# Strassen's seven products for three quarters of the MLP's way down, sums kept in SBUF

## The chip, the cores and the metric

One core of one Trainium2 chip runs the whole program in one launch. The metric is device time in microseconds, the median of three runs. Five engines with queues of their own matter: TensorE (PE; its weight loads are listed as PEld), VectorE (DVE), ScalarE (ACT), GpSimd (POOL, which issues weight loads) and SyncE (SP, which issues the other transfers).

## The reference, cut to what matters

Two layers on 512 tokens of width 1024. Each is a mixer (three attention branches, gates, an output projection) and an MLP with a hidden width of 4096:

```
x = x + mixer(rmsnorm(x, g_mix[l])) 
h = rmsnorm(x, g_mlp[l])
x = x + square(relu(h @ w_up[l])) @ w_down[l]     # 1024 -> 4096 -> 1024
```

After the second layer comes a last RMSNorm. All inputs are float32. The change touches `@ w_down[l]`, what feeds it and what takes its result.

## The kernel before, in words

Activations lie channel-major: a tile has 128 channels on the partitions and the 512 tokens (`S`) along the row. Every float32 product is made of three matmuls in fp32r: each operand is split into a high part (a ScalarE copy with rounding) and a low part (a VectorE subtraction), and `mm3` adds high*high, high*low and low*high in PSUM. `wblock` loads a block of weights of 128 x 1024 words through POOL's queue into a `raw` tile and splits it into a pair of `w` tiles.

The program isn't issued in the order in which it is written. `Plan` records every operation, and `Plan.schedule` (line 306) then places them by a list schedule with costs of its own: on each engine the ready operation that was written earliest goes first, if its tiles fit. SBUF has 42 slots of 1024 words and 12 of 512 (`n4`, `n2`), PSUM has 8 banks. The limits that matter here: at most 12 `w` tiles and 6 `raw` tiles at once, and a `raw` load at most 350 recorded operations ahead of the first one that isn't placed yet (`limits`, `ahead`). A tile is given a slot only if the operations written before it still find room for theirs (`fits`). Every instruction is emitted from one line, 562, so groups are told apart by tile names.

The MLP (from `mark("mlp")`, line 1546) runs in two halves of the hidden width. In each, 16 chunks of 128 hidden channels are made: 24 matmuls of 512 columns on `h`, a Relu on ScalarE, a product on VectorE that makes the square, and the split into `u` (in slots tagged co, qk, om, v). Then, for each pair of 128-channel output blocks (`mp` 0 to 3), four blocks of `w_down` are loaded and split, two PSUM banks take 48 matmuls of 512 columns each, and VectorE multiplies by the norm's factor `R2` and adds to the residual `xt`, which lies in SBUF from the output projection (`mark("wout")`) on. In the second half of the last layer the last pair is done by halves of 256 tokens, so that the end of the program overlaps with matmuls. The inner loop of the way down reads:

```
for q in range(2):
    for i in range(2):
        wh, wl = wblock(w_down[l], 16 * hf + 8 * q, 8, 256 * mp + 128 * i)
        mm3(pp[i], wh, wl, us[8 * q:8 * q + 8], first=q == 0, last=q == 1)
```

Of the kernel before, what the change touches and what calls it, by code (L numbers as in the profile page):

```python
# [12 lines left out]
F32R = mybir.dt.float32r  # L13
I32 = mybir.dt.int32
AF = mybir.ActivationFunctionType
OP = mybir.AluOpType
# [4 lines left out]
S = 512  # L21
# [7 lines left out]
for _n, _w in ([("dq", 512), ("dk", 512), ("dv", 512)]  # L29
# [13 lines left out]


class View:
# [530 lines left out]
def trunk(ctx, tc, x, w_in, b_gate, g_mix, diff_lambda, g_diff, g_cq, g_ckv, w_uq, w_ukv,  # L576
# [9 lines left out]
    ten, act, dve = plan.tensor, plan.scalar, plan.vector  # L586

    def mark(label):
        plan.label = label
        plan.boost = opts["boost"] if label == "A" else 0  # L590
    plan.boost = 0

    def T(tag, shape=None, dt=F32):
        if shape is None:
            shape = dict(t=[128, S], th=[128, S], o=[128, S], p=[128, S], pd=[128, 1024], raw=[128, 1024]).get(tag, [128, 2, S])
        return plan.tile(shape, dt, tag)

    def H(tag):
        return T(tag, [128, 2, S], F32R)
# [4 lines left out]
    def P(tag, shape=(128, S)):  # L604
        return plan.bank(shape, tag)

    def dma(dst, src):
        return plan.sync.dma_start(dst, src)

    def copy(dst, src, scale=1.0):  # L610
        return act.activation(dst, src, AF.Copy, scale=scale)
# [17 lines left out]
    p = P("mm")  # L629
# [5 lines left out]
    def load(src, kc, n):  # L635

        v = T("raw")[:, :kc * n].rearrange("p (k n) -> p k n", n=n)
        plan.gpsimd.dma_start(v, src)
        return v

    def wview(w, k0, kc, c0, n):
        return w[k0 * 128:(k0 + kc) * 128, c0:c0 + n].rearrange("(k p) n -> p k n", p=128)

    def pair():

        wh = T("w", [128, 1024], F32R)
        wl = T("w", [128, 1024], F32R)
        plan.together(wh, wl)
        return wh, wl
# [24 lines left out]

    def hilo(dst, src):
        copy(dst[:, 0], src)
        dve.tensor_sub(dst[:, 1], src, dst[:, 0])
# [60 lines left out]
    xs = [plan.dram(dr.tile([128, 2, S], F32, name=f"xs{k}")) for k in range(4)]  # L738
    h = [None] * KD
# [45 lines left out]
    for k in range(KD):  # L785
        p = P("x0")
# [39 lines left out]
    def layer(l, norm):  # L826
# [59 lines left out]
        k0 = 0  # L886
        for kc in (3, 3, 2):
            wh, wl = wblock(W, k0, kc, LAY["ckv"], 288)
            for k in range(kc):
                for b in range(4):  # L890
                    a0, a1 = (h[k0 + k][:, u, 128 * b:128 * b + 128] for u in range(2))
                    o = p4[b][:, :288]
# [9 lines left out]
        s4 = small(4)  # L902
# [8 lines left out]
        r2, v, f = small(4), small(4), small(4)  # L911
# [10 lines left out]
        for k in range(2):  # L922
            p = P("tp")
            for b in range(4):
                ten.transpose(p[:, 128 * b:128 * b + 128], u4[:, b, 128 * k:128 * k + 128], ident)
            c = H("co")
            g = gckv[:, k:k + 1]
# [5 lines left out]
        for a, op in ((0, dve.tensor_sub), (1, dve.tensor_add)):  # L933
            o = kro[:, :, 16 * a:16 * a + 16]
# [3 lines left out]
        p = P("tp")  # L938
# [30 lines left out]
        for pr in range(4):  # L969
            p = P("mm")  # L970
            mm3(p, khw, klw, ckv, c0=128 * pr)
            t = H("rx")
# [25 lines left out]
        for b in range(4):  # L998
            p = P("mm")
            vproj(p, vhw, vlw, ckv, b, 512)  # L1000
            src = p.rearrange("p (r h d) -> p r h d", h=2, d=64)
# [481 lines left out]
        g = {br: [(f"g{br}{m}", 1.0, bind(gate, br, m)) for m in range(8)] for br in range(3)}  # L1483
# [45 lines left out]
        merged = [merged[m] for m in range(KD)]  # L1529

        mark("wout")
        xt = []
        for i in range(4):
            t = T("xt", [128, 2, S])
            dma(t, xs[i])
            xt += [t[:, 0], t[:, 1]]
        n2 = Norm(gmlp)
        for mp in range(4):
            for i in range(2):
                m = 2 * mp + i  # L1540
                wh, wl = wblock(w_out[l], 0, 8, 128 * m)
                p = P("mm")
                mm3(p, wh, wl, merged)
                dve.tensor_add(xt[m], xt[m], p)
                n2.chunk(m, xt[m])
        mark("mlp")
        last = l == NL - 1
        nn = Norm(vec(g_final if last else g_mix[l + 1], KD))
        R2 = None
        for hf in range(2):  # L1550
            us = []
            for jp in range(8):
                for i in range(2):
                    wh, wl = wblock(w_up[l], 0, 8, 2048 * hf + 256 * jp + 128 * i)
                    p = P("mm")
                    mm3(p, wh, wl, h)
                    t = T("t")
                    act.activation(t, p, AF.Relu)
                    dve.scalar_tensor_tensor(t, p, 0.0, t, OP.max, OP.mult)
                    n = len(us)  # L1560
                    u = H("co" if n < 4 else "qk" if n < 10 else "om" if n < 14 else "v")
                    hilo(u, t)
                    us.append(u)
                if hf == 0 and jp == 0:
                    Rt2 = n2.stat(DM)
                    sq = small(4)
                    dve.tensor_mul(sq, Rt2, Rt2)
                    R2 = R
                    copy(R2, spread(sq))
            for mp in range(4):  # L1570
                if last and hf == 1 and mp == 3:
                    break
                pp = [P("mm"), P("mm")]
                for q in range(2):
                    for i in range(2):
                        wh, wl = wblock(w_down[l], 16 * hf + 8 * q, 8, 256 * mp + 128 * i)
                        mm3(pp[i], wh, wl, us[8 * q:8 * q + 8], first=q == 0, last=q == 1)
                for i in range(2):
                    m = 2 * mp + i
                    t = T("t")  # L1580
                    dve.tensor_mul(t, pp[i], R2)
                    dve.tensor_add(xt[m], xt[m], t)
                    if hf == 1:
                        if last:
                            nn.sq(xt[m])
                        else:
                            dma(xs[m // 2][:, m % 2], xt[m])
                            nn.chunk(m, xt[m])
        if not last:
            return nn  # L1590

# [1 line left out]
        for k in range(6):  # L1593
            copy(xt[k], xt[k], scale=nn.g[:, k:k + 1])
        orow = out[0].rearrange("(p r) d -> r p d", r=4)
        ws = [[wblock(w_down[l], 16 + 8 * q, 8, 128 * m) for m in (6, 7)] for q in range(2)]
        for hh in range(2):
            cs = slice(256 * hh, 256 * hh + 256)
            pp = [P("mm")[:, :256], P("mm")[:, :256]]
            for q in range(2):  # L1600
                for i in range(2):
                    mm3(pp[i], *ws[q][i], [u[:, :, cs] for u in us[8 * q:8 * q + 8]], first=q == 0, last=q == 1)
            sums = [nn.acc]
            for i in range(2):
                xm = xt[6 + i][:, cs]
                t = T("t")
                dve.tensor_mul(t[:, cs], pp[i], R2[:, cs])
                dve.tensor_add(xm, xm, t[:, cs])
                sq = T("t")
                act.activation(sq[:, cs], xm, AF.Square)  # L1610
                copy(xm, xm, scale=nn.g[:, 6 + i:7 + i])
                sums.append(sq)
            p = P("tp")
            for n, sq in enumerate(sums):
                for j in range(2):
                    c = 256 * hh + 128 * j
                    ten.matmul(p[:, j:j + 1], sq[:, c:c + 128], ones, start=n == 0 and j == 0, stop=n == 2 and j == 1)
            v = small(2)
            dve.tensor_scalar(v, p[:, 0:2], 1.0 / DM, EPS, op0=OP.mult, op1=OP.add)
            y = rsqrt(v, 2)  # L1620
            for j in range(2):
                r = 2 * hh + j
                ot = T("v", [128, 2, S])
                for q in range(2):
                    p = P("x0")
                    for k in range(4):
                        ten.transpose(p[:, 128 * k:128 * k + 128], xt[4 * q + k][:, 128 * r:128 * r + 128], ident)
                    if q == 0:
                        copy(ot[:, q], p, scale=y[:, j:j + 1])
                    else:  # L1630
                        dve.tensor_scalar(ot[:, q], p, y[:, j:j + 1], None, op0=OP.mult)
                    dma(orow[r][:, S * q:S * q + S], ot[:, q])
# [58 lines left out]
```

## Time and profile before

| what | value |
|---|---|
| runs | 2001.65, 1988.54, 1996.59 us; median 1996.59 |
| the profiled execution | 2001.1 us, span 1999.3 us |
| mean granted TensorE clock | 0.991 |
| instructions | 25782, of them 9652 matmuls |
| busy PE, DVE, ACT, POOL | 1949.1, 1249.1, 836.6, 219.8 us |

In the profile a matmul's recorded end is modelled and matmuls are pipelined, so the pace of a stream is read from start to start in the timeline, not from the mean of one. An engine that is busy all the time shows in a stage's window; an engine's idle time matters only where another one waits for it.

### The profile page before, as it was taken

The page shows a single profiled execution, that of the slowest core. Times are in us where ns is not written, and L with a number is a line of the kernel's source. Part 1 is how long each engine was busy: PE and PEld are TensorE (multiplying, and loading weights), DVE is VectorE, ACT ScalarE, POOL GpSimd, SP SyncE. Part 2 cuts the span into 40 slices and gives each one's busy share as a digit, 9 for nine tenths or more (in the row PEclk, how much of TensorE's full clock was granted, in tenths as well). Part 3 has the DMA queues.
Part 4 walks back from the last instruction along what each step waited for, and adds up shares of the span by engine and source line. Part 5 has one row for each costly group of instructions (what it writes and reads, how often), then busy time and mean ns, then how long its engine had stood idle before and what let it go on. Part 6 is the DMA issues. An engine that isn't in the chain of part 4 may idle for free.

```text
span 1999.3 us, 25782 instructions
## 1 busy us (share of the span) xinstructions
PE 1949.1 (97%) x9652; PEld 1620.4 (81%) x9652; DVE 1249.1 (62%) x2633; ACT 836.6 (42%) x1539; POOL 219.8 (11%) x260
## 2 busy tenths in 40 slices
PE   8899899999999999999999999999999999999998
PEld 7788788887778888888887877888877888888887
DVE  6687867788866533444356977687878754334432
ACT  5465544544434431333243754455434433223321
POOL 1000001000111111211100000001011211111100
PEclk9999999999999999999999999999999999999999
DMA  7944626567653323433257264456667433234211
GB/s 219 200 112 139 188 76 188 166 159 208 171 158 102 97 74 94 117 90 110 79 119 187 72 188 129 127 148 177 167 190 219 130 86 103 74 107 115 83 55 43
DMA packets 191220, 263.17 MB, mean 132 GB/s; under 512 B 97964, under 2 KB 128684, under 8 KB 191096
## 3 DMA queue, kind: packets, MB, share of 16 engines
q1 hardware_dynamic: 154776, 129.14, 24.1%
q0 software_dynamic: 36320, 132.40, 23.4%
q8 instruction: 76, 1.25, 0.3%
q14 instruction: 48, 0.39, 0.1%
HBM read 210.83 MB, written 46.47 MB: 129 GB/s over the span
## 4 chain that ended last, share of the span: by engine, by line
PE 85%; DMA 7%; DVE 5%; ACT 1%; SPq 1%; issue 1%; DVEq 0%; ACTq 0%
PE mm L562 74%; PE s L562 4%; PE tp L562 3%; PE av L562 3%; DMA raw<-in_w_in_dram 2%; DMA raw<-in_w_uq_dram 1%; SPq L562 1%; DVE t L562 1%; DMA sm<-al 1%; DVE w L562 1%; DVE sm L562 1%; DMA al<-sm 1%; DVE oo L562 1%; DVE rx L562 1%; ACT w L562 0%
## 5 line engine op out<-in xcount | busy, mean ns | idle before, releaser
L562 PE MATMUL mm<-h,w 128*128 128x512 f32 x3936 | 970.2, 398 | 0.0
L562 PEld LDWEIGHTS mm<-h,w 128*128 128x128 f32 x3936 | 731.9, 189 | 160.1 <-issue 0.3
L562 DVE TENSOR_TENSOR w<-raw,w 128x1024 fp32r<-128x1024 f32 (+4 forms) x366 | 372.9, 1031 | 120.4 <-ACT w L562 118.2
L562 ACT ACTIVATE w<-raw 128x1024 fp32r<-128x1024 f32 (+4 forms) x366 | 321.9, 901 | 210.0 <-PE mm L562 123.3
L562 PE MATMUL mm<-co,w 128*128 128x512 f32 (+1 forms) x864 | 212.0, 392 | 3.7 <-ACT w L562 3.1
L562 PE MATMUL mm<-qk,w 128*128 128x512 f32 (+1 forms) x900 | 212.0, 385 | 0.0
L562 PE MATMUL mm<-om,w 128*128 128x512 f32 (+1 forms) x792 | 194.9, 388 | 0.0
L562 PEld LDWEIGHTS mm<-qk,w 128*128 128x128 f32 x900 | 164.6, 188 | 36.1
L562 PEld LDWEIGHTS mm<-co,w 128*128 128x128 f32 x864 | 158.5, 189 | 39.5 <-ACT w L562 3.5
L562 DVE TENSOR_TENSOR t<-mm,const 128x512 f32<-128x512 f32 (+1 forms) x114 | 75.3, 677 | 182.3 <-PE mm L562 181.9
L562 PEld LDWEIGHTS mm<-om,w 128*128 128x128 f32 x792 | 144.7, 188 | 32.0 <-issue 0.2
L562 POOL DMA_DIRECT2D raw<-in_w_in_dram x86 | 74.9, 873 | 855.8 <-PE mm L562 313.9
L562 PE MATMUL mm<-w,h 128*128 128x256 f32 (+1 forms) x1152 | 155.8, 287 | 0.0
L562 PEld LDWEIGHTS mm<-w,h 128*128 128x128 f32 x1152 | 149.7, 191 | 3.6 <-DVE w L562 0.4
L562 PE MATMUL s<-qk,qk 96*128 96x512 f32 (+2 forms) x448 | 128.0, 371 | 8.0 <-DVE sm L562 4.2
L562 DVE SCALAR_TENSOR_TENSOR t<-mm,t 128x512 f32<-128x512 f32 x64 | 44.2, 691 | 141.1 <-ACT t L562 141.1
L562 ACT ACTIVATE t<-mm 128x512 f32<-128x512 f32 x74 | 44.2, 597 | 189.8 <-PE mm L562 189.8
L562 ACT ACTIVATE p<-s,sm 128x512 f32<-128x512 f32 x128 | 87.1, 684 | 63.3 <-DVE sm L562 62.9
L562 ACT ACTIVATE pt<-tp 128x512 fp32r<-128x512 f32 x128 | 71.7, 595 | 87.5 <-PE tp L562 85.1
L562 PE MATMUL av<-pt,v 128*128 128x256 f32 x576 | 98.3, 293 | 5.6 <-DVE pt L562 3.4
L562 PEld LDWEIGHTS av<-pt,v 128*128 128x128 f32 x576 | 83.4, 191 | 22.2 <-DVE pt L562 8.0
L562 PEld LDWEIGHTS s<-qk,qk 128*128 128x128 f32 (+1 forms) x448 | 81.3, 192 | 23.5 <-DVE sm L562 5.6
(141 smaller groups left out, 1717.4 us busy)
## 6 DMA issues: line engine op xcount, KB each, us to landing
raw<-in_w_in_dram POOLq DMA_DIRECT2D x80, 512.0 KB, 6.3
raw<-in_w_up_dram POOLq DMA_DIRECT2D x64, 512.0 KB, 4.8
raw<-in_w_down_dram POOLq DMA_DIRECT2D x64, 512.0 KB, 4.8
dk<-rx SPq DMA_DIRECT2D x40, 512.0 KB, 4.9
qk<-dk SPq DMA_DIRECT2D x40, 512.0 KB, 6.5
raw<-in_w_in_dram SPq DMA_DIRECT2D x24, 512.0 KB, 6.8
dq<-rx SPq DMA_DIRECT2D x40, 256.0 KB, 4.5
qk<-dq SPq DMA_DIRECT2D x20, 512.0 KB, 4.4
```

The lines of the kernel that those rows point to most:

```text
L562: getattr(getattr(self.nc, op.eng), op.m)(*args, **kw)
```

## The change

The hidden width of each layer is cut in four quarters. For the first three (`PAIRS = (4, 4, 4)`: three groups of four pairs of hidden chunks) the way down is computed by the Strassen-Winograd scheme. A block problem has two halves of hidden channels (the two chunks of a pair), two halves of output channels (the two blocks of an `mp`) and two halves of tokens. Eight products of 256 columns become seven, made from sums of weight blocks (`ss`) and of activation blocks (`ht`), each of which is split into high and low parts again. The seven products lie in four PSUM banks; after each group they are copied (first group) or added (second and third) into tiles in SBUF (`da`, `db`). `outputs` combines them at the end. The last quarter is done as before, with eight chunks. The residual is written to DRAM in the output projection and read back before the last quarter (`x_back`).

```diff
+PAIRS = (4, 4, 4)
...
+        xm, xt = x_back()
...
+            dma(xs[mp], xm[mp])
...
+        def up_pair(c0):
+            b = T("hb", [128, 2, 2, HB])
+            for i in range(2):
+                wh, wl = wblock(w_up[l], 0, 8, c0 + 128 * i)
+                p = P("mm")
+                mm3(p, wh, wl, h)
+                t = T("t")
+                act.activation(t, p, AF.Relu)
+                act.activation(b[:, i].rearrange("p t n -> p (t n)"), t, AF.Square)
+            t13, t24 = T("ht", [128, 2, HB]), T("ht", [128, 2, HB])
+            dve.tensor_sub(t13[:, 0], b[:, 0, 1], b[:, 0, 0])
+            dve.tensor_sub(t13[:, 1], b[:, 1, 1], b[:, 0, 1])
+            dve.tensor_sub(t24[:, 0], b[:, 1, 1], t13[:, 0])
+            dve.tensor_sub(t24[:, 1], t24[:, 0], b[:, 1, 0])
+            parts = []
+            for src in (b[:, :, 0], t13, t24):
+                u = T("u", [128, 2, 2, HB], F32R)
+                copy(u[:, 0], src)
+                dve.tensor_sub(u[:, 1], src, u[:, 0])
+                parts += [u[:, :, 0], u[:, :, 1]]
...
+            hilo(u, b[:, 1, 1])
+            b11, b21, t1, t3, t2, t4 = parts
+            return [b11, b21, u, t4, t1, t2, t3]
+
+        def down_weights(k0, n, mp):
+            rows = w_down[l][128 * k0:128 * k0 + 256 * n, 256 * mp:256 * mp + 256].rearrange("(j i p) n -> p i j n", i=2, p=128)
+            raw = [load(rows[:, i], n, 256).rearrange("p j (o n) -> p j o n", o=2) for i in range(2)]
...
+            s12, s34 = four(T("ss", [128, 1024])), four(T("ss", [128, 1024]))
+            dve.tensor_add(s12[:, 0], raw[0][:, :, 1], raw[1][:, :, 1])
+            dve.tensor_sub(s12[:, 1], s12[:, 0], raw[0][:, :, 0])
+            dve.tensor_sub(s34[:, 0], raw[0][:, :, 0], raw[0][:, :, 1])
+            dve.tensor_sub(s34[:, 1], raw[1][:, :, 0], s12[:, 1])
+            wh, wl = pair()
+            a1 = [four(w) for w in (wh, wl)]
+            for i in range(2):
+                copy(a1[0][:, i], raw[i][:, :, 0])
+                dve.tensor_sub(a1[1][:, i], raw[i][:, :, 0], a1[0][:, i])
+            a2 = four(T("w", [128, 1024], F32R))
+            copy(a2[:, 0], raw[1][:, :, 1])
+            dve.tensor_sub(a2[:, 1], raw[1][:, :, 1], a2[:, 0])
+            ws = []
+            for s_ in (s12, s34):
+                wh, wl = pair()
+                copy(four(wh), s_)
+                dve.tensor_sub(four(wl), s_, four(wh))
...
+        def product(o, n, ws, us):
+            wh, wl = ws[n]
+            for j, u in enumerate(us):
+                u0, u1 = u[n][:, 0], u[n][:, 1]
+                ten.matmul(o, wh[:, j], u0, start=j == 0, stop=False)
+                ten.matmul(o, wh[:, j], u1, start=False, stop=False)
+                ten.matmul(o, wl[:, j], u0, start=False, stop=j == len(us) - 1)
+
+        BANKS = ((0, 1), (5, 6), (3, 4), (2,))
...
+        def keep(g, mp, pb):
...
+                if g == 0:
+                    copy(d, p)
+                else:
+                    dve.tensor_add(d, d, p)
+
+        def outputs(mp):
+            c = T("hb", [128, 2, 2, HB])
+            p12, p67, p45, p3 = sums[mp]
+            dve.tensor_add(c[:, 0, 0], p12[:, 0], p12[:, 1])
+            dve.tensor_add(p12[:, 0], p12[:, 0], p67[:, 0])
+            dve.tensor_add(p67[:, 0], p12[:, 0], p67[:, 1])
+            dve.tensor_add(p12[:, 0], p12[:, 0], p45[:, 1])
+            dve.tensor_sub(c[:, 1, 0], p67[:, 0], p45[:, 0])
+            dve.tensor_add(c[:, 0, 1], p12[:, 0], p3)
+            dve.tensor_add(c[:, 1, 1], p12[:, 0], p67[:, 1])
...
+        for g, n in enumerate(PAIRS):
+            us = []
+            for j in range(n):
+                us.append(up_pair(256 * (first + j)))
...
+            for mp in range(4):
+                keep(g, mp, down(2 * first, n, mp, us))
+            first += n
+
+        us = [up_chunk(128 * c) for c in range(2 * first, 32)]
+        first *= 2
+        xm, xt = x_back()
+        for mp in range(4):
+            cs = outputs(mp)
+            for i in range(2):
+                m = 2 * mp + i
+                dve.tensor_mul(cs[i], cs[i], R2)
+                dve.tensor_add(xt[m], xt[m], cs[i])
+        for mp in range(4):
+            if last and mp == 3:
+                break
+            pp = [P("mm"), P("mm")]
+            for i in range(2):
+                wh, wl = wblock(w_down[l], first, len(us), 256 * mp + 128 * i)
+                mm3(pp[i], wh, wl, us)
...
-        ws = [[wblock(w_down[l], 16 + 8 * q, 8, 128 * m) for m in (6, 7)] for q in range(2)]
+        ws = [wblock(w_down[l], first, len(us), 128 * m) for m in (6, 7)]
```

## Rows read from the trace of the kernel before

**Rows 1.** Page, span and engines: busy us (share of the span), instructions.
```profile
span 1999.3 us, 25782 instructions
...
PE 1949.1 (97%) x9652; PEld 1620.4 (81%) x9652; DVE 1249.1 (62%) x2633; ACT 836.6 (42%) x1539; POOL 219.8 (11%) x260
```

**Rows 2.** Page, the chain that ended last: shares of the span by engine.
```profile
PE 85%; DMA 7%; DVE 5%; ACT 1%; SPq 1%; issue 1%; DVEq 0%; ACTq 0%
```

**Rows 3.** Windows of layer 0's MLP: stretch, its us, busy us, clock, DMA, GB/s.
```profile
655.00:745.00 90.00, 90.00 (x393) 72.82 (x392) 39.51 (x61) 33.02 (x47) 11.73 (x14) 1.00 0.30 82
...
745.00:835.00 90.00, 90.00 (x390) 72.91 (x389) 33.91 (x37) 20.51 (x21) 16.77 (x19) 1.00 0.40 110
```

**Rows 4.** Timeline of PE, 512-column matmuls on the way down: start us, us, count.
```profile
985.45 2.94 PE L562 MATMUL mm<-qk,w 128*128 128x512 f32 x12
988.23 2.93 PE L562 MATMUL mm<-co,w 128*128 128x512 f32 x12
991.00 4.34 PE L562 MATMUL mm<-qk,w 128*128 128x512 f32 x18
```

**Rows 5.** Timeline of PE, 256-column matmuls on the way down, near the end.
```profile
1978.38 1.58 PE L562 MATMUL mm<-qk,w 128*128 128x256 f32 x12
1979.80 1.58 PE L562 MATMUL mm<-co,w 128*128 128x256 f32 x12
```

**Rows 6.** Groups by form, PE, whole span: busy us, mean ns, idle before.
```profile
L562 PE MATMUL mm<-w,h 128*128 128x256 f32 x960 | 127.9, 283 | 0.0
```

**Rows 7.** Timeline of DVE in the output projection, instructions back to back.
```profile
596.99 0.68 DVE L562 SCALAR_TENSOR_TENSOR th<-th,mm 128x512 f32<-128x512 f32 x1
597.70 0.69 DVE L562 TENSOR_TENSOR co<-co,th 128x512 f32<-128x512 f32 x1
...
598.91 1.22 DVE L562 TENSOR_TENSOR w<-raw,w 128x1024 fp32r<-128x1024 f32 x1
600.04 0.68 DVE L562 SCALAR_TENSOR_TENSOR qk<-co,qk 128x512 fp32r<-128x512 f32 x1
600.65 0.68 DVE L562 TENSOR_TENSOR co<-co,th 128x512 f32<-128x512 f32 x1
```

**Rows 8.** Groups by form, DVE, whole span: a 256-column operation.
```profile
L562 DVE TENSOR_TENSOR t<-s,const 128x256 f32<-128x256 f32 x32 | 12.6, 418 | 1.9 <-PE s L562 1.8
```

**Rows 9.** Groups by form, ACT, 680 to 1000 us.
```profile
L562 ACT ACTIVATE w<-raw 128x1024 fp32r<-128x1024 f32 x54 | 56.3, 1053 | 65.9 <-PE mm L562 61.1 <-issue 4.8
...
L562 ACT ACTIVATE qk<-t 128x512 fp32r<-128x512 f32 x11 | 7.0, 632 | 8.3 <-DVE t L562 8.3
```

**Rows 10.** Timelines of ACT and DVE: from a hidden chunk's matmuls to its `u`.
```profile
676.85 0.60 ACT L562 ACTIVATE t<-mm 128x512 f32<-128x512 f32 x1 [2.52 <-PE mm L562]
678.20 0.63 ACT L562 ACTIVATE qk<-t 128x512 fp32r<-128x512 f32 x1 [0.76 <-DVE t L562]
...
678.87 0.69 DVE L562 TENSOR_TENSOR qk<-t,qk 128x512 fp32r<-128x512 f32 x1 [0.70 <-ACT qk L562]
```

**Rows 11.** DMA issues: count, KB each, median us from issue to landing.
```profile
raw<-in_w_down_dram POOLq DMA_DIRECT2D x64, 512.0 KB, 4.8
...
xt<-xs SPq DMA_DIRECT2D x8, 512.0 KB, 6.7
```

**Rows 12.** Waits, 650 to 1000 us: who for whom, us, times, longest us.
```profile
POOL raw L562 <- DVE w L562: 245.5, 50, 13.1
...
DVE w L562 <- ACT w L562: 34.6, 34, 4.4
```

**Rows 13.** Groups by form, DVE, 680 to 1000 us, with releasers.
```profile
L562 DVE TENSOR_TENSOR w<-raw,w 128x1024 fp32r<-128x1024 f32 x54 | 65.7, 1223 | 35.7 <-ACT w L562 33.8 <-issue 1.0 <-PE mm L562 0.8
...
L562 DVE TENSOR_TENSOR t<-mm,const 128x512 f32<-128x512 f32 x15 | 10.4, 692 | 75.3 <-PE mm L562 75.3
```

**Rows 14.** Windows, a stretch of layer 0's mixer in which PE was starved.
```profile
240.00:260.00 20.00, 15.71 (x66) 12.77 (x65) 8.88 (x18) 9.71 (x18) 0.00 (x0) 0.83 0.39 128
```

More of the change, by code (lines that the diff above doesn't have):

```diff
@@ L1531, in layer, with x_back @@
         mark("wout")
[L1532 to L1536, printed above, removed]
+        def x_back():
+            ts = [T("xt", [128, 2, S]) for _ in range(4)]
+            for i in range(4):
+                dma(ts[i], xs[i])
+            return ts, [t[:, i] for t in ts for i in range(2)]
+        xm, xt = x_back()
         n2 = Norm(gmlp)
@@ L1549, in layer @@
         R2 = None
-        for hf in range(2):
-            us = []
[L1552 to L1564, printed above, removed]
+        HB = S // 2
@@ new lines, in layer @@
+        sums = {}
+        def up_pair(c0):
[18 more added lines that the diff above has]
+                parts += [u[:, :, 0], u[:, :, 1]]
+            if "u" not in sums:
+                sums["u"] = T("u", [128, 2, 2, HB], F32R)
+                u = sums["u"][:, 0]
+            else:
+                u = sums.pop("u")[:, 1]
+            hilo(u, b[:, 1, 1])
+            b11, b21, t1, t3, t2, t4 = parts
+            return [b11, b21, u, t4, t1, t2, t3]
@@ new lines, in down_weights, with four @@
+        def down_weights(k0, n, mp):
+            rows = w_down[l][128 * k0:128 * k0 + 256 * n, 256 * mp:256 * mp + 256].rearrange("(j i p) n -> p i j n", i=2, p=128)
+            raw = [load(rows[:, i], n, 256).rearrange("p j (o n) -> p j o n", o=2) for i in range(2)]
+            def four(t):
+                return t[:, :256 * n].rearrange("p (a j n) -> p a j n", a=2, n=128)
+            s12, s34 = four(T("ss", [128, 1024])), four(T("ss", [128, 1024]))
[16 more added lines that the diff above has]
+                dve.tensor_sub(four(wl), s_, four(wh))
+                ws += [(four(wh)[:, a], four(wl)[:, a]) for a in range(2)]
+            s1, s2, s3, s4 = ws
+            return [(a1[0][:, 0], a1[1][:, 0]), (a1[0][:, 1], a1[1][:, 1]), s4, (a2[:, 0], a2[:, 1]), s1, s2, s3]
@@ new lines, in product, with down @@
+        def product(o, n, ws, us):
[6 more added lines that the diff above has]
+        BANKS = ((0, 1), (5, 6), (3, 4), (2,))
+        def down(k0, n, mp, us):
+            ws = down_weights(k0, n, mp)
+            pb = []
+            for ns in BANKS:
+                p = P("x0", [128, 2, HB])
+                for k, i in enumerate(ns):
+                    product(p[:, k], i, ws, us)
+                pb.append(p)
+            return pb
@@ new lines, in keep @@
+        def keep(g, mp, pb):
+            if g == 0:
+                t = T("da", [128, 2, 2, HB])
+                if mp == 0:
+                    sums["w"] = T("da", [128, 4, HB])
+                sums[mp] = [t[:, 0], t[:, 1], T("db", [128, 2, HB]), sums["w"][:, mp]]
+            for k in range(4):
+                d, p = sums[mp][k], pb[k] if k < 3 else pb[k][:, 0]
+                if g == 0:
+                    copy(d, p)
+                else:
+                    dve.tensor_add(d, d, p)
@@ new lines, in outputs @@
+        def outputs(mp):
[8 more added lines that the diff above has]
+            dve.tensor_add(c[:, 1, 1], p12[:, 0], p67[:, 1])
+            return [c[:, o].rearrange("p t n -> p (t n)") for o in range(2)]
@@ new lines, in up_chunk @@
+        def up_chunk(c):
+            wh, wl = wblock(w_up[l], 0, 8, c)
+            p = P("mm")
+            mm3(p, wh, wl, h)
+            t = T("t")
+            act.activation(t, p, AF.Relu)
+            dve.scalar_tensor_tensor(t, p, 0.0, t, OP.max, OP.mult)
+            u = H("u")
+            hilo(u, t)
+            return u
+        first = 0
+        for g, n in enumerate(PAIRS):
+            us = []
+            for j in range(n):
+                us.append(up_pair(256 * (first + j)))
+                if g == 0 and j == 0:
@@ L1570, in layer @@
             for mp in range(4):
[L1571 to L1588, printed above, removed]
+                keep(g, mp, down(2 * first, n, mp, us))
[16 more added lines that the diff above has]
+                mm3(pp[i], wh, wl, us)
+            for i in range(2):
+                m = 2 * mp + i
+                t = T("t")
+                dve.tensor_mul(t, pp[i], R2)
+                dve.tensor_add(xt[m], xt[m], t)
+                if last:
+                    nn.sq(xt[m])
+                else:
+                    dma(xs[m // 2][:, m % 2], xt[m])
+                    nn.chunk(m, xt[m])
         if not last:
@@ L1599, in layer @@
             pp = [P("mm")[:, :256], P("mm")[:, :256]]
-            for q in range(2):
-                for i in range(2):
-                    mm3(pp[i], *ws[q][i], [u[:, :, cs] for u in us[8 * q:8 * q + 8]], first=q == 0, last=q == 1)
+            for i in range(2):
+                mm3(pp[i], *ws[i], [u[:, :, cs] for u in us])
             sums = [nn.acc]
```

## The prediction

> **What bounds the kernel now.** The page comes first: PE is busy for 97% of the span, DVE for 62% [rows 1], and 85% of the chain that ended last is PE [rows 2]. That is a mean over stages, so the windows of the MLP come next [rows 3]: PE is busy for all of each 90 us, DVE for 38 to 44% of it, ACT for 23 to 37%, at full clock, and no wait of PE is listed in that stage. So in the MLP, which is all that the change touches, time is matmuls in a stream. DVE and ACT are covered until one of them needs more time per unit of work than PE does. A stream's pace is read from start to start: 24 matmuls of 512 columns take 991.00 - 985.45 = 5.55 us, 231.3 ns each [rows 4]; 12 of 256 columns take 1.42 us, 118.3 ns each [rows 5]. Half the columns cost 51% of the time, though each matmul has its own weight load.
>
> **PE's part.** A pair of hidden chunks and an output pair (`mp`) took 4 blocks x 3 = 12 matmuls of 512 columns, 12 x 231.3 = 2.776 us; now it takes 7 products x 3 = 21 of 256, 21 x 118.3 = 2.484 us. There are 12 pairs x 4 `mp` x 2 layers = 96 of them: 266.5 - 238.5 = 28.0 us less. All else of PE's work (way up, last quarter) stays, but for 96 of the 192 narrow matmuls at the end, which the count above holds as wide ones; that is under 1 us. Bounds: 118.3 ns is the lower end for a narrow matmul; the upper is the group in the mixer, 127.9 / 960 = 133.2 ns [rows 6], by which the saving would be 266.5 - 268.5 = -2 us. I take 118.3: it is the same kind of stream (`w` stationary, a hidden tile moving), while the mixer's group is broken up by other work.
>
> **DVE's part.** Now the cover. A call of `down` (one group, one `mp`) is 84 matmuls, 9.94 us of PE. DVE's prices, start to start: 1024 words 1.13 us, 512 words 0.61 us, and 0.71 us where the next one reads its result [rows 7]; 256 words at most 0.42 us [rows 8]. A call's weights take four sums and three low parts of 512 words, and two low parts of 1024: 7 x 0.61 + 2 x 1.13 = 6.5 us, where two blocks took 2 x 1.13 = 2.3 us for the same columns. In groups two and three `keep` adds 3 x 0.61 + 0.42 = 2.25 us, so 8.8 us of 9.94: DVE is 88% busy there (16 calls in all), and 65% in the first group, where ACT copies instead. ACT's part of a call, by its durations [rows 9], is 2 x 1.05 + 3 x 0.63 = 4.0 us, 2.2 more with the copies. On the way up a pair is 48 x 231.3 = 11.1 us of PE; DVE has two weight blocks (2.3), four sums of 256 (1.7), three low parts of 512 and one of 256 (2.25), 6.2 us; ACT 2 x 1.05 + 7 x 0.63 + 0.4 = 6.9 us. So each engine stays under PE, and I cost all this at nothing; in the later groups its cover is 1.1 us a call.
>
> **At each group's start.** The products need the last pair at once, where the old accumulation came to the last chunk at its end. From Relu to the stored low part the old path took 679.56 - 676.85 = 2.7 us [rows 10], and the new one (Relu, Square, copy, low part) has steps of the same kind. Meanwhile PE has the first three pairs in four banks, 4 x 9 x 0.118 = 4.3 us, if the call's weights stand; with only the first bank's ready, 2.1 us. The sums `t1` to `t4` of the last pair come some 3 us later (four dependent subtractions at 0.46 at most, a copy, a low part) and can show 0 to 1.5 us. I take 0.8 us for each of the 6 groups, 5 us; bounds 0 and 6 x 2.5 = 15.
>
> **Loads and slots.** POOL issues as many loads (24 calls x 2 + 16 = 64 for `w_down`, as before, with rows twice as long), 4.8 us to landing [rows 11]. POOL already waits for `raw` slots most of the time, 245.5 us of this stage for DVE alone [rows 12], and PE never felt it. In a call 14 `u`, 8 `h` and 5 `da` tiles leave 15 of the 42 slots; a call needs 2 `raw`, 2 `ss` and 7 `w`, and 7 `w` of the next fit beside its own 7. The loads for the call after that go out when the first bank's weights are released, 2.8 us into the call, land 0.9 + 4.8 us later, and have until the end of the next call: some 11 us for 6.5 of sums plus 2.25 of `keep`. It fits, with 2 us over: nothing at the centre, and see the second rival.
>
> SP gets four writes of the residual and four reads more per layer. A read takes 6.7 us to landing [rows 11] against 44 us of the last quarter's way up; behind the writes wait the norm's small transfers, whose result `R2` is now not needed until `outputs`: nothing. `outputs` and its products are 4 x (7 x 0.42 + 4 x 0.61) = 21 us of DVE beside eight chunks of 5.55 us whose own DVE work is 2.35 us each: 40 of 44 us, covered. At the end 48 narrow matmuls instead of 96 cover the first half's output: up to 1 us.
>
> **The sum.** -28.0 + 5 + 1 = -22 us. The profiled execution took 2001.1 us (span 1999.3), which gives 1979. It lies 4.5 us above the median 1996.6, so on the scale of the median I forecast 1975 us.
>
> **Rivals.**
>
> First, on the slow side: DVE becomes the bound in the 16 later calls. In this stage it stood still for ACT's high part for 33.8 us in 54 blocks, 0.63 us each [rows 13]. That happened while it had little else to do; if its fixed order brings the same wait before each of a call's five low parts, the call takes 8.8 + 3.1 = 11.9 us, 16 x 2.0 = 31 us over PE's, and the gain is gone (1996.6 - 28 + 31 = 2000). If, besides, no two instructions overlap, the durations count in full (0.69, 1.22, 0.42): 10 x 0.69 + 2 x 1.22 + 0.42 + 3.1 = 12.9 us, 16 x 2.9 = 47 us, 2016 us, slower by 1%. It decides from 11.7 us a call on. For it: the margin of 1.1 us; `keep` also waits for PE's last product, with the next call's low parts behind it on DVE. Against it: the placing puts other ready work first, and independent instructions start 0.61 us apart though they last 0.68 [rows 7]. The Trainium skill, "VectorE: DVE Perf Modes", section "The DRAIN you can't avoid", states that the next instruction does not start until the pipe is empty; by that rule the full durations are the price, and a call takes 9.8 us even without ACT's waits, no cover at all. This trace agrees only where the next one reads the result (0.71 us), so the rule doesn't set the sum.
>
> Second: weights come late. The margin of 2 us per call is one slow landing; if each of the 24 calls shows 3 us (2.4 us of sums and a copy behind a late load), that is 72 us, 2041. A PE that starves also loses clock: in a starved stretch of 20 us it was granted 0.83, so part of it ran at 1.2 instead of 2.4 GHz [rows 14]. Against it: PE waited for no load in this stage.
>
> Third: the change doesn't give what it says, because narrow matmuls in this place go at the mixer's 133.2 ns [rows 6]: -2 + 6, 2000 us. Against it: the stream near the end [rows 5].
>
> Fourth: part of the gain goes, with DVE late in some later calls (0.5 to 1 us in each of 16) and the group starts at their upper bound: 8 to 20 us left, 1977 to 1989.
>
> **Chances and range.** My forecast (stalls of 0 to 12 us, 1968 to 1981) 0.60; the fourth 0.17; the first 0.15, half of it at 2000 and half beyond; the third 0.03; the second 0.05. About 1% (20 us, so 1976.6 and 2016.6) is what this measurement tells from no change. Faster by over 1%: three quarters of the forecast's 0.60 and a little of the fourth, 0.48. Slower by over 1%: the second and the far half of the first, 0.13. Within 1%: 0.39. The range reaches from no stall at all (1996.6 - 28 - 3 for the spread of the runs, 1966) up to the first rival's near half, 2000; it leaves out nearly 0.2.
>
> **What would show it.** Right: 2016 matmuls of 256 columns on `u`, starting some 118 ns apart; under 10 us of PE waiting on `w` and `u` in both MLPs; the MLP stages some 11 us shorter each; DVE 85 to 90% busy in the later groups' way down. DVE's rival: PE idle before `mm` for DVE's `w` or for banks, DVE over 95% busy or waiting for ACT. The second: waits for `raw` landings or a PE clock under 1 in the MLP. The third: starts 133 ns apart with no wait. I am wrong in kind if the MLP stages get longer, or if the mixers, which are not touched, move by more than the runs' spread of 13 us.

## The result: 1.2 to 1.4% faster, nearly the whole of TensorE's saved columns

The changed kernel took 1968.44 us (median of 4) against 1997.89 us, a ratio of 0.986 with a 95% interval of 0.982 to 0.990. Run again on another occasion it took 1970.92 us (median of 6) against 1995.07 (of 17), 0.9876 (0.9853 to 0.9898). The forecast was 1975 us in a range of 1966 to 2000. The medians below leave out two single executions, one of the kernel with short products (2217 us) and one of that with fourteen pairs (6674 us), which took far longer than the others of the same kernel.

The page after, its span and engines, which answers to [rows 1]:

```profile
span 1966.6 us, 28095 instructions
...
PE 1917.2 (97%) x10468; PEld 1637.1 (83%) x10468; DVE 1425.8 (73%) x3017; ACT 943.4 (48%) x1739; POOL 213.6 (11%) x260
```

There are more instructions on each of PE, DVE and ACT, and PE is busy for 32 us less, while DVE gained 177 us and ACT 107. The span is 32.7 us shorter. The stages show where these went. PE's timeline gives the marks: the first matmul of the way up in each layer, the first of layer 1's projection of 288 columns, and the last matmul on weights. In us:

| kernel | to layer 0's MLP | MLP 0 | layer 1's mixer | MLP 1 | end |
|---|---|---|---|---|---|
| before | 647.9 | 357.0 | 623.3 | 360.0 | 11.2 |
| before, again | 642.2 | 357.0 | 627.7 | 360.0 | 11.2 |
| changed | 638.7 | 343.4 | 625.7 | 347.7 | 11.2 |
| changed, again | 640.4 | 343.4 | 628.1 | 346.1 | 11.2 |
| an eighth product | 640.6 | 360.1 | 623.0 | 363.1 | 11.7 |
| residual in SBUF | 640.8 | 343.5 | 623.9 | 348.1 | 11.2 |
| the same, 39 slots | 649.6 | 355.0 | 635.8 | 360.8 | 11.2 |
| late writes | 638.6 | 343.0 | 620.6 | 346.5 | 11.2 |
| low parts twice | 641.4 | 343.0 | 623.5 | 345.9 | 11.1 |
| low parts three times | 644.7 | 351.8 | 623.6 | 354.8 | 11.8 |
| low parts four times | 636.8 | 393.3 | 630.1 | 393.4 | 11.7 |
| short products | 641.4 | 300.4 | 630.6 | 305.2 | 11.8 |
| fourteen pairs | 642.1 | 339.7 | 634.2 | 344.9 | 12.4 |

With fourteen pairs the mark between MLP 0 and the mixer comes early: ten matmuls of the MLP stand behind it, and with them MLP 0 is 342.1 us and the mixer 631.7.

The MLPs repeat within 0.1 us between two profiles of the kernel before and within 1.6 us between two of the changed one. They got 25.9 us shorter in the first pair and 27.5 us in the second. The two mixers together move by several us from one execution to the next, which is the rest of the 32.7 us.

PE's timeline of layer 0's MLP after, which answers to [rows 4, 5] (start us, us, what, count):

```profile
684.42 39.78 PE L565 MATMUL x<-u,w 128*128 128x256 f32 x336
724.03 44.79 PE L565 MATMUL mm<-h,w 128*128 128x512 f32 x192
768.66 39.94 PE L565 MATMUL x<-u,w 128*128 128x256 f32 x336
808.43 44.73 PE L565 MATMUL mm<-h,w 128*128 128x512 f32 x192
853.00 40.05 PE L565 MATMUL x<-u,w 128*128 128x256 f32 x336
892.90 44.75 PE L565 MATMUL mm<-h,w 128*128 128x512 f32 x192
937.49 44.71 PE L565 MATMUL mm<-u,w 128*128 128x512 f32 x192
```

A group's four calls are 336 narrow matmuls in 724.03 - 684.42 = 39.61 us, 117.9 ns each, and 118.4 and 118.8 in the later groups. No bracket with an idle time stands in any row, so PE did not stop between these matmuls. The windows of the same stretches answer to [rows 3] (stretch, its us, busy us and count of PE, PEld, DVE, ACT and POOL, clock, DMA share, GB/s):

```profile
684.42:724.03 39.61, 39.61 (x337) 39.61 (x336) 23.28 (x28) 25.88 (x39) 8.59 (x10) 1.00 0.45 118
724.03:768.66 44.63, 44.63 (x195) 36.06 (x193) 24.86 (x42) 21.33 (x36) 3.00 (x4) 1.00 0.21 69
768.66:808.43 39.77, 39.77 (x337) 39.77 (x336) 34.33 (x49) 20.14 (x26) 10.09 (x12) 1.00 0.45 127
808.43:853.00 44.57, 44.57 (x194) 36.07 (x193) 25.60 (x44) 20.78 (x34) 2.99 (x4) 1.00 0.24 76
853.00:892.90 39.90, 39.90 (x338) 39.89 (x336) 36.01 (x57) 19.20 (x25) 8.58 (x10) 1.00 0.49 132
892.90:937.49 44.59, 44.59 (x194) 36.07 (x193) 37.39 (x61) 17.28 (x23) 7.82 (x9) 1.00 0.47 142
```

DVE is busy for 59% of the first group's way down and 86 and 90% of the later ones, and PE for all of each. The first line below is the group of narrow matmuls on the new tiles (busy us, mean ns of one, idle before it): it waited 0.3 us in all. The two lines behind it are all the waits of PE in layer 1's MLP (who for whom, us, times, longest):

```profile
L565 PE MATMUL x<-u,w 128*128 128x256 f32 x2016 | 239.9, 281 | 0.3 <-DVE u L565 0.3
```

```profile
PE tp L565 <- DVE sm L565: 1.3, 1, 1.3
PE x L565 <- DVE u L565: 0.3, 1, 0.3
```

### The profile page after: what moved, and what is told of

It reads as the page before. It is cut to its first block, busy times and chain, and to the rows that moved or that the text cites. A ratio compares the mean times of both kernels' runs of the same rounds, so it can differ in the third digit from the quotient of the medians.

```text
span 1966.6 us, 28095 instructions
## 1 busy us (share of the span) xinstructions
PE 1917.2 (97%) x10468; PEld 1637.1 (83%) x10468; DVE 1425.8 (73%) x3017; ACT 943.4 (48%) x1739; POOL 213.6 (11%) x260
## 4 chain that ended last, share of the span: by engine, by line
PE 78%; DMA 9%; DVE 8%; issue 3%; ACT 1%; SPq 1%; DVEq 0%; ACTq 0%; POOLq 0%
PE mm L565 56%; PE x L565 12%; PE s L565 4%; PE av L565 3%; DMA raw<-in_w_in_dram 3%; PE tp L565 3%; DVE w L565 2%; DVE t L565 1%; DVE sm L565 1%; DMA sm<-al 1%; SPq L565 1%; DMA al<-sm 1%; DMA raw<-in_w_uq_dram 1%; DVE oo L565 1%; DVE rx L565 1%
## 5 line engine op out<-in xcount | busy, mean ns | idle before, releaser
L565 DVE TENSOR_TENSOR w<-raw,w 128x1024 fp32r<-128x1024 f32 (+3 forms) x390 | 362.7, 945 | 74.0 <-ACT w L565 63.0
L565 ACT ACTIVATE w<-raw 128x1024 fp32r<-128x1024 f32 (+3 forms) x390 | 314.8, 831 | 170.0 <-DMA raw<-in_w_in_dram 57.2
L565 PEld LDWEIGHTS x<-u,w 128*128 128x128 f32 x2016 | 239.5, 189 | 1.0 <-DVE u L565 0.5
L565 PE MATMUL x<-u,w 128*128 128x256 f32 x2016 | 239.9, 281 | 0.3 <-DVE u L565 0.3
L565 PE MATMUL mm<-co,w 128*128 128x512 f32 x456 | 117.1, 402 | 4.5 <-ACT w L565 4.1
L565 DVE TENSOR_TENSOR t<-mm,const 128x512 f32<-128x512 f32 (+1 forms) x98 | 64.3, 675 | 58.3 <-PE mm L565 57.9
L565 PEld LDWEIGHTS mm<-co,w 128*128 128x128 f32 x456 | 85.0, 191 | 23.9 <-ACT w L565 4.5
L565 PE MATMUL mm<-om,w 128*128 128x512 f32 x384 | 100.3, 396 | 0.0
L565 DVE TENSOR_REDUCE sm<-s 128x1 f32<-128x512 f32 x128 | 86.2, 683 | 19.3 <-PE s L565 18.9
L565 PE MATMUL mm<-u,w 128*128 128x512 f32 (+1 forms) x432 | 89.9, 369 | 0.0
```

Source lines behind the costliest of these rows:

```text
L565: getattr(getattr(self.nc, op.eng), op.m)(*args, **kw)
```

## The experiments

Two theories stood against each other at first: that the gain is the columns that PE no longer streams, with all else under its cover, and that part of it comes from elsewhere (the mixers, the residual's freed slots, the longer rows of the loads). Behind them stood the two rivals of the prediction, which say how thick the cover is: DVE, and the slots.

**The changed kernel again**, no edit.

> The changed kernel once more, nothing edited. Theory (columns): the gain is TensorE's columns alone, 28.0 us counted, 25.9 us in the MLPs of the profiled pair; the other 6.8 us of that pair (layer 0's mixer 9.3 us earlier, layer 1's 2.4 us later, with the same instructions in the same order in layer 0) is spread from run to run. Then the MLPs take 343 and 348 us again within 1 us, layer 0's MLP starts anywhere from 638 to 648 us, and the ratio is about 0.987. Rival (elsewhere): the change also speeds the mixer or the loads; then layer 0's MLP starts at 638 to 639 us again and the ratio is about 0.983.

Measured: 1970.92 us, ratio 0.9876; the MLPs 343.4 and 346.1 us. Layer 0's came back as the columns theory has it; layer 1's is 1.6 us shorter than in the first profile, where "within 1 us" was expected. PE's stops there, of 1.29 and 0.28 us in the first profile, are one of 0.32 us here. Layer 0's MLP began at 640.4 us, outside what the rival expected, but not far enough to settle the mixer.

**The kernel before again**, for its profile.

> The kernel before once more, for its profile. Theory: the mixers are not touched; layer 0's MLP starts anywhere from 638 to 648 us (the one profile of before shows 647.9, five of changed kernels 638.6 to 640.8, with the same instructions in the same order until then), its MLPs take 357 and 360 us again. Rival: the change moves the mixer by 8 us; then this profile shows 646 to 650 us again.

Measured: layer 0's MLP began at 642.2 us, 5.7 us earlier than in the first profile of the same kernel, and its MLPs took 357.0 and 360.0 us again. So most of the mixers' 6.8 us in the first pair is spread between executions. (PE's first 3326 matmuls, of which 3230 lie ahead of layer 0's MLP, are of the same kinds in the same order before and after.) Two profiles of the kernel before can't exclude that the change moves the mixers by a us or two.

**An eighth product.**

```diff
-        BANKS = ((0, 1), (5, 6), (3, 4), (2,))
+        BANKS = ((0, 1), (5, 6), (3, 4), (2, 2))
```

> The last of the seven products is computed a second time into the free half of its bank, so a call has 96 narrow matmuls instead of 84; sums, splits, copies, adds and slots stay. Theory (columns): 12 matmuls x 24 calls x 118.3 ns = 34 us come back, 2002 us, 0.2 to 0.4% over the kernel before, because eight narrow products cost 6 us more than the wide ones did. Rival (elsewhere: freed slots of the residual, longer rows of the loads, the mixers): part of the gain stays, 1985 to 1995 us.

Measured: 2007.41 us, 36.5 over the changed kernel of the same session; ratio to before 1.0057 (1.0038 to 1.0076). The MLPs took 360.1 and 363.1 us, 16.8 and 16.9 over the changed kernel's: 33.7 us for 288 matmuls, 117 ns each. Against the kernel before they are 3.2 and 3.1 us longer, 6.2 us, which is what eight narrow products cost over four wide ones by the two paces. With all the rest of the change in place and only one product's matmuls given back, the gain is gone. This is the proof for the columns. The times lie 12.3 us over the kernel before, where 6 were expected; the profiled execution was the fastest of ten (2000.62 us), and where the other 6 us lie in the slower ones stays open.

**The residual stays in SBUF.**

```diff
-            dma(xs[mp], xm[mp])
...
         first *= 2
-        xm, xt = x_back()
```

> The residual stays in SBUF through the MLP as before the change: no write in the output projection, no second read; 4 slots fewer for weights, 11 instead of 15. Theory: by the count of slots a call needs 11 (2 raw, 2 ss, 7 w), so the next call's weights can start only as the first bank's are released, 2.8 us into a call; 0.9 + 5.0 us to landing and 3 us to the first split pair make 11.7 us against 9.94 us of TensorE, so 1.8 us of waiting in each of 24 calls, 43 us: about 2010 us, with TensorE waits on w in both MLPs. Rival: slots are not scarce, the writes and reads are not needed: within 3 us of the changed kernel, and TensorE shows no wait.

Measured: 1972.52 us, ratio 0.9883 (0.9854 to 0.9912), no slower than the changed kernel; MLPs 343.5 and 348.1 us. My count of slots fell: PE's waits for `w` are 1.1 us in all, in the first groups, where I had 43. Windows of the later groups' way down in this kernel (columns as above):

```profile
771.28:811.06 39.78, 39.78 (x338) 39.77 (x336) 35.81 (x53) 20.02 (x26) 10.82 (x13) 1.00 0.45 130
855.49:895.31 39.82, 39.82 (x337) 39.81 (x336) 36.42 (x57) 19.20 (x26) 10.07 (x12) 1.00 0.44 123
```

PE is busy for all of both. A call does not hold its 11 tiles at one time. In DVE's timeline of the first of these stretches one call reads a `raw` tile for the last time 3 us before it splits its second `ss` tile into the last pair of `w`:

```profile
782.31 0.69 DVE L565 TENSOR_TENSOR w<-raw,w 128x512 fp32r<-128x512 f32 x1
...
785.51 1.22 DVE L565 TENSOR_TENSOR w<-ss,w 128x1024 fp32r<-128x1024 f32 x1
```

That slots which come free so early are the reason why four fewer cost nothing was not tested by itself. The spill of the residual to DRAM, which the change brings along, buys nothing that the runs can tell, and costs nothing either.

**The same with 39 slots** (in `opts`).

```diff
-n2=12, n4=42
+n2=12, n4=39
```

> As with the residual kept in SBUF, and 39 slots of 1024 words instead of 42, so 8 are left for weights in the later groups of a call instead of 15. Theory: with 11 no wait showed, since raw and sum tiles are free again before the next call's splits stand; with 8, fewer than the 11 tiles that a call has in all, the next call's weights can't be begun until most of a call is over: 2 us or more in each of 16 later calls, 30 us or more, 2000 us and over; also fewer slots in the mixers, whose own loss can be told apart by the stages. Rival: still no wait in the MLP.

Measured: 2017.11 us, ratio 1.0100 (1.0074 to 1.0125). The MLPs grew by 11.5 and 12.7 us over the kernel with 42 slots and the residual in SBUF, 24.2 us where 30 or more were expected, and the mixers by 8.8 and 11.9. PE's timeline of the second group's way down (idle before it and releaser in brackets):

```profile
781.08 10.16 PE L565 MATMUL x<-u,w 128*128 128x256 f32 x84
791.81 0.50 PE L565 MATMUL x<-u,w 128*128 128x256 f32 x2 [0.56 <-ACT w L565]
792.53 10.54 PE L565 MATMUL x<-u,w 128*128 128x256 f32 x84 [0.23 <-DVE w L565]
804.50 0.50 PE L565 MATMUL x<-u,w 128*128 128x256 f32 x2 [1.43 <-ACT w L565]
805.58 11.89 PE L565 MATMUL x<-u,w 128*128 128x256 f32 x96 [0.58 <-DVE w L565]
```

PE does about a call's 84 matmuls and then waits for the next call's first weights, call after call. So weights do come late when slots are short, as the second rival has it, but seven slots away from the changed kernel, and four of them cost nothing.

**The residual's writes behind the norm.**

```diff
-            dma(xs[mp], xm[mp])
...
                     copy(R2, spread(sq))
+                    for k in range(4):
+                        dma(xs[k], xm[k])
```

> The four writes of the residual come behind the norm's small transfers (after the first pair of hidden chunks) instead of ahead of them. Theory: the 1.29 us that TensorE waited in layer 1 before the four transposes that spread the norm's factor is the norm's small transfers standing behind the writes in SyncE's queue; the wait goes to 0 and layer 1's MLP gets 1.3 us shorter, which the times alone can't show (0.07%). Rival: the wait is the norm's own chain, and stays at 1 us or more.

Measured: 1966.44 us, ratio 0.9857 (0.9831 to 0.9883), and no wait of PE before the four transposes of layer 1; in the changed kernel's first profile that row was the only longer stop of PE in either MLP:

```profile
1632.84 0.65 PE L565 MATMUL tp<-const,sm 128*128 128x128 f32 x4 [1.29 <-DVE sm L565]
```

That fits, but doesn't prove the queue: in the changed kernel's second profile the same wait is 0.32 us, and with the residual in SBUF, so with no writes at all, it is 0.36. The transposes were also placed earlier among the matmuls here. What sets this wait stays open; it is worth 1.3 us at most. This version has the lowest median of those that do the whole work, by less than the runs can tell.

**DVE's cover: low parts twice, three times, four times.** The edit for two; for three and four the line stands once and twice more. `Plan` knows the cost of the added subtractions and places all operations anew, so each dose also changes the order on every engine.

```diff
                 dve.tensor_sub(four(wl), s_, four(wh))
+                dve.tensor_sub(four(wl), s_, four(wh))
```

> The two low parts of 1024 words of each call are subtracted twice, 2 x 1.13 = 2.27 us more of VectorE in each of the 24 calls, nothing else. Theory (VectorE is close under TensorE): the 16 later calls need 8.7 + 2.3 = 11.0 us against 9.94, the 8 first ones 8.1; 16 x 1.1 = 17 us slower than the changed kernel, or some less as each group's first call is prepared on the way up: 10 to 17 us, with TensorE waiting for VectorE in the later groups and none in the first. Rival (VectorE has room, by working ahead through the way up): under 3 us.

> The two low parts of 1024 words of each call are subtracted three times, 4.54 us more of VectorE per call than in the changed kernel. Three counts of VectorE's cover: per call (13.2 us in a later call against 9.94, 11.0 in a first one: 61 us slower than the changed kernel); per group with the first call's weights made on the way up (4 x 13.2 - 11 = 41.9 us against 39.8, so 2 us in each of 4 later groups, 8 us); over a whole group, way up and way down together (4 x 6.2 + 4 x 13.2 = 78 us against 84, nothing). I hold the second.

> The same low parts subtracted four times, 6.8 us more of VectorE per call. Per call: 15.5 us against 9.94 and 13.3 against 9.94, 116 us slower. Per group with one call ahead: 4 x 15.5 - 13.3 = 48.7 us against 39.8, 9 us in each of 4 later groups and none in the first, 36 us slower. Over a whole group: 4 x 6.2 + 4 x 15.5 = 87 us against 84, 12 us slower. I hold the second; TensorE's waits for w and for u in the later groups' way down should add up to it.

Measured, beside the changed kernel's MLPs of 343.4 and 346.1 us in its second profile: twice, 1966.74 us, MLPs 343.0 and 345.9, no loss; three times, 1988.13 us, 351.8 and 354.8, 17.1 us lost; four times, 2065.30 us, 393.3 and 393.4, 97 us lost. The second group's way down in each of the three, as a window (columns as above):

```profile
771.17:812.33 41.16, 41.16 (x343) 40.91 (x342) 39.61 (x55) 21.41 (x27) 8.57 (x10) 1.00 0.42 116
```

```profile
775.14:824.97 49.83, 47.60 (x364) 45.00 (x363) 48.33 (x63) 22.42 (x29) 8.56 (x10) 1.00 0.36 97
```

```profile
772.84:837.49 64.65, 51.57 (x347) 49.70 (x346) 56.19 (x68) 21.93 (x28) 9.45 (x12) 0.84 0.29 82
```

With two, DVE is busy for 96% of the stretch and PE for all of it. By the count per call (8.7 + 2.3 = 11.0 us against 9.94) 17 us should have been lost. The timeline shows how it was avoided:

```profile
771.17 34.98 PE L565 MATMUL x<-u,w 128*128 128x256 f32 x294
805.99 1.32 PE L565 MATMUL mm<-h,w 128*128 128x512 f32 x5
807.15 2.77 PE L565 MATMUL x<-u,w 128*128 128x256 f32 x22
```

PE takes 294 matmuls, three calls and a half, without a stop, which is more than DVE could prepare beside them by that count; so part of their weights was made ahead, on the way up. And before the last products it takes six matmuls of the next way up. So the cover is not 1.1 us a call. It isn't the whole group's mean either, which I had as the third count: with three, DVE is busy for 97% of the stretch and PE waits, 17 us lost where one call of work ahead had said 8 and the mean nothing. With four, 97 us are lost, where one call ahead had said 36 and the count per call 116. The waits alone are 60.0 us, as the group of narrow matmuls shows (busy us, mean ns, idle before it), and the first group's way down, where no loss was expected, took 46.99 us instead of 39.6:

```profile
L565 PE MATMUL x<-u,w 128*128 128x256 f32 x2016 | 274.9, 301 | 60.0 <-DVE w L565 51.3 <-ACT w L565 8.7
```

The same group is also busy for 274.9 us instead of 239.9, and the windows say why: the granted clock of the second group's stretch is 0.84, so part of it ran at 1.2 GHz instead of 2.4. Two of PE's rows with the stop before each, and two windows of the same work:

```profile
783.52 7.57 PE L565 MATMUL x<-u,w 128*128 128x256 f32 x62 [1.21 <-ACT w L565]
794.30 11.53 PE L565 MATMUL x<-u,w 128*128 128x256 f32 x72 [3.21 <-DVE w L565]
```

```profile
783.52:790.90 7.38, 7.38 (x62) 7.38 (x62) 7.02 (x10) 2.60 (x3) 0.89 (x1) 1.00 0.20 71
794.30:800.40 6.10, 6.09 (x28) 6.10 (x29) 4.42 (x6) 2.21 (x3) 0.00 (x0) 0.50 0.18 61
```

After the stop of 1.21 us 62 matmuls took 7.38 us at full clock, 119 ns each; after the one of 3.21 us 28 took 6.10 us at half of it, some 215 ns each. DVE, the engine that PE waits for, is busy for 87% of the stretch only: it waits for PE's products in turn, 5.8 us before the adds of `keep`.

**Short products.**

```diff
-                    product(p[:, k], i, ws, us)
+                    product(p[:, k], i, ws, us if i in (0, 1, 3) else us[:1])
```

> Products 2, 4, 5 and 6 (by the list's numbers) take only the first of the four pairs, so a call has 36 + 12 = 48 narrow matmuls instead of 84; this leaves out part of the way down. All sums, splits and adds stay. Theory: VectorE now sets the pace, 8.7 us in a later call and 6.5 in a first one, where TensorE needs 5.7: 16 x (9.94 - 8.7) + 8 x (9.94 - 6.5) = 47 us less than the changed kernel, 1924 us. Rival (VectorE far from the bound): 36 x 24 x 118.3 ns = 102 us less, 1868 us.

Measured: 1891.11 us, ratio 0.9482 (0.9447 to 0.9516); MLPs 300.4 and 305.2, 83.9 us less than the changed kernel's, between the 47 of DVE's pace and the 102 of PE's. The first group lost nothing; the later groups' way down lost 4.2 us each against PE's pace (28.8 us, of which 1.9 are matmuls of the next way up, for 22.7):

```profile
754.35 8.39 PE L565 MATMUL x<-u,w 128*128 128x256 f32 x64
762.92 0.74 PE L565 MATMUL x<-u,w 128*128 128x256 f32 x4 [0.18 <-ACT w L565]
763.87 10.28 PE L565 MATMUL x<-u,w 128*128 128x256 f32 x80 [0.21 <-ACT w L565]
773.98 1.71 PE L565 MATMUL mm<-h,w 128*128 128x512 f32 x6
777.38 5.21 PE L565 MATMUL x<-u,w 128*128 128x256 f32 x42 [1.69 <-DVE w L565]
```

Neither count holds: PE does wait for DVE and ACT in the later groups, as theory had it, but the loss against PE's pace is 18 us where the count per call had 55. Work done ahead is the likely cover for the rest.

**Fourteen pairs.** With the late writes; `PAIRS = (4, 4, 4, 2)`.

```diff
-PAIRS = (4, 4, 4)
+PAIRS = (4, 4, 4, 2)
```

> Fourteen of sixteen pairs by seven products (a fourth group of two pairs), the last four chunks in the old way, and the residual's writes behind the norm's small transfers. TensorE: 2 pairs x 4 x 2 layers x 0.292 = 4.7 us less than the changed kernel. Theory: the group of two pairs needs 5.9 us of VectorE per call against 5.0 of TensorE, and the outputs' 21 us now have four chunks (22 us) instead of eight beside them; if the cover is counted over a stretch, as the doubled low parts suggest, both MLPs get 2 us shorter each and the end of the program 1 to 2 us longer. Rival (the end of each layer turns to VectorE's pace): the MLPs get longer than 343 and 346 us.

Measured: 1972.42 us, ratio 0.9884 (0.9857 to 0.9910). Once more, for a trace:

> Fourteen pairs once more, for a trace: the profiled execution of the first try was disturbed. Its times (1972 to 1976 us against 1962 to 1976 of the same kernel with twelve) speak for the rival. Theory: both MLPs 2 us shorter than 343.0 and 346.5 us, the end of the program longer. Rival: VectorE's pace at the end of each layer, where the outputs' 21 us have four chunks beside them; then layer 0's MLP is no shorter than 343 us and TensorE or the next layer's start waits there.

Measured: 1975.08 us in one run. Layer 1's MLP took 344.9 us, 1.6 less than with twelve pairs and late writes; layer 0's took 342.1 us with its ten late matmuls, 0.9 less; the end 12.4 us, 1.3 more; the mixer between them 631.7 us, where the other profiles with 42 slots have 620.6 to 630.6. PE's timeline at the start of layer 1:

```profile
981.77 0.29 PE L565 MATMUL mm<-w,h 128*128 128x288 f32 x1
981.90 2.47 PE L565 MATMUL mm<-u,w 128*128 128x512 f32 x10
...
984.61 0.63 PE L565 MATMUL mm<-h,w 128*128 128x512 f32 x2
988.88 5.96 PE L565 MATMUL mm<-w,h 128*128 128x288 f32 x25 [3.64 <-DVE w L565]
```

Windows of the last four chunks' way up, of the way down behind them, and of the matmuls after the stop (columns as above):

```profile
938.74:961.03 22.29, 22.29 (x98) 18.06 (x97) 22.29 (x47) 9.06 (x14) 1.91 (x3) 1.00 0.24 74
961.03:984.21 23.18, 22.59 (x99) 18.11 (x97) 22.57 (x40) 12.88 (x20) 6.40 (x8) 1.00 0.60 178
988.88:994.10 5.22, 5.22 (x22) 5.22 (x23) 4.11 (x7) 3.37 (x6) 0.88 (x1) 0.50 0.46 147
```

Each theory had a part of it. The MLPs got shorter, though by less than 2 us. But DVE is busy for all of the last four chunks, beside which the outputs now have to be done, and for nearly all of the way down behind them, so the next layer's first weights are late. PE stops for 3.6 us and runs at half its clock afterwards. That and the longer end give more back than the 2.5 us gained. This is one profile; the ratios with and without the fourth group (0.9884 and 0.9857) have intervals that overlap, so no gain of the fourth group is shown, and no loss either.

## Why the prediction was right

**PE's part, -28.0 us.** It was the whole story: the MLPs gave 25.9 and 27.5 us. The pace of narrow matmuls held, 117.9 to 118.8 ns against the 118.3 read from twelve matmuls at the end of the trace before [rows 5], so taking it over the mixer's 133.2 ns [rows 6] was right; the third rival is out. The eighth product shows that nothing else in the MLPs adds to the gain.

**The groups' start, +5 us.** Mis-sized: 0.3 us in all, one wait of 0.28 us for `u` in layer 1's first group. It did not end with the sums `t1` to `t4`, for which I had up to 1.5 us: what ended it is the low part of the last pair's own blocks (`hb`), on DVE.

```profile
1657.38 0.68 DVE L565 TENSOR_TENSOR u<-hb,u 128x512 fp32r<-128x512 f32 x1
```

```profile
1658.12 36.89 PE L565 MATMUL x<-u,w 128*128 128x256 f32 x310 [0.28 <-DVE u L565]
```

In the other five groups PE had work until the last pair was there.

**The end, +1 us.** It was 0.0 (11.2 us before and after).

**DVE's cover.** The busy shares came out as counted (59% and 86 to 90%, forecast 65 and 88), and "nothing" was right as a cost. What failed is the step behind it, "its cover is 1.1 us a call", and with it the first rival's point of 11.7 us a call, from which the gain was to be gone: 2.3 us more in each call (11.0) cost nothing, and with 4.5 us more (13.2) the kernel was still faster than before, 0.9952 (0.9933 to 0.9970). Work done ahead covers more than the margin of a call. How much is not settled: one call ahead, the nearest of the three counts, has 0, 8 and 36 us for the three doses, and 0, 17 and 97 were lost, the last partly by the clock. The first rival's mechanism did not show: DVE's waits for ACT's high parts in the whole second group, four calls, are 0.6 us, where the rival had 3.1 in each call (who for whom, us, times, longest):

```profile
DVE w L565 <- ACT w L565: 0.6, 3, 0.3
```

The Trainium skill, "VectorE: DVE Perf Modes", section "The DRAIN you can't avoid", says that the next operation does not start until the pipe is empty, and adds that one that is not held starts earlier; the prediction left out that addition. DVE's timeline of a later group is in line with that addition for neighbours that don't depend on each other:

```profile
861.08 0.69 DVE L565 TENSOR_TENSOR ss<-ss,raw 128x512 f32<-128x512 f32 x1
861.75 0.69 DVE L565 TENSOR_TENSOR db<-db,x 128x512 f32<-128x512 f32 x1
862.36 1.29 DVE L565 TENSOR_TENSOR w<-raw,w 128x512 fp32r<-128x512 f32 x2
863.56 0.41 DVE L565 TENSOR_TENSOR da<-da,x 128x256 f32<-128x256 f32 x1
```

862.36 - 861.75 = 0.61 us where one lasts 0.69, so 0.08 us of overlap.

**Loads and slots.** "It fits, with 2 us over" was too narrow: four slots fewer cost nothing, seven cost 24 us in the MLPs, less than half of the second rival's 72. I had counted the tiles of a call as if all were held together.

**SP's queue, nothing.** Nearly: PE waited 1.29 us for the norm's factor in one profile and 0.32 in the other. I had said that nobody needs `R2` before `outputs`; its four transposes stand in PE's queue, in order, with the way up behind them. What sets that wait is open.

**The sum.** -22 us was forecast, -24 to -29 measured. The allowance of 6 us for stops was the part that was off. On the scale of single executions, with the 2 us by which the first pair's MLPs fell short of PE's 28.0, 2001.1 - 28 + 2 = 1975; the profiled execution took 1968.35, and the other 6.8 us are the mixers', which no term of the sum held.

## What to carry to other kernels

Where one engine is busy without a gap, count its work in the pace of a stream of the same kind, read from start to start, and take work off it even if another engine gains more than five times as much, as long as that engine stays covered. Then check the cover over the cycle in which work can be done ahead, not call by call, and find its end by adding work to the covering engine in doses. Busy shares of 96, 97 and 87% on the covering engine went with losses of 0, 17 and 97 us here: the share alone doesn't tell these apart, a wait on the covered engine does. And a saving at the end of a stage can be given back if it removes what the next stage's start was hidden behind, as one profile showed.

## What the runs showed of the hardware that was not expected

A stream of 256-column matmuls, each with a weight load of its own, kept PE at 118 ns per matmul with the row of weight loads busy for all of the stretch (39.61 of 39.61 us), against 81% with 512 columns (36.06 of 44.63): a full row of weight loads was no slowdown. And some stops cost more than themselves: after 3.2 us with low parts four times, and after 3.6 us with fourteen pairs, PE's next matmuls ran at a granted clock of 0.50, narrow ones some 215 ns apart instead of 118; after a stop of 1.21 us the clock was still 1.00.
